# A hybrid decoder block: small matmuls of even and odd heads issued in alternation, each half in its own PSUM bank

## The chip, the cores and the metric

The kernel runs on one core of one Trainium2 chip. The metric is the device time of one execution in microseconds (us). Times of single instructions and stages come from one profiled execution of that core. TensorE is called PE, its weight loads PEld, VectorE DVE, ScalarE ACT, GpSimd POOL and SyncE SP.

## What is computed

One decoder block over 512 tokens and 16 learned meta tokens, width 1024, all in float32. A mixer runs two kinds of heads side by side, stick-breaking attention (8 heads of 64) and gated linear attention (GLA, 4 heads with keys of 64 and values of 128), and one output projection joins them. Behind it a PEER layer looks up 16 of 16384 one-neuron experts for each of 8 heads and token.

```python
# stick-breaking attention, per head
z = einsum('qd,kd->qk', q, k) * 64 ** -0.5
log_1m = where(mask, log_sigmoid(-z), 0)
between = cumsum(log_1m, reverse=True) - log_1m
a = where(mask, exp(log_sigmoid(z) + between), 0);  o = a @ v
# gated linear attention, per head and chunk
o = (q * exp(bcum)) @ state + (q k^T with decay exp(bcum_t - bcum_s), causal) @ v
state = exp(b_last) * state + (k * exp(b_last - bcum))^T @ v
# PEER
s1, s2 = q1 @ sub_keys1^T, q2 @ sub_keys2^T     # per head, 64 features, 128 keys each
top 16 of each, top 16 of the sums, softmax -> gates
y = sum_k gate_k * gelu(x . U[e_k]) * V[e_k]
```

## The kernel before

The 512 tokens are four blocks of 128 in two groups: blocks 0 to 2 (group 0) and block 3 (group 1). `front(g)` is the mixer of a group and `mid(g)` its output projection, second norm and PEER queries. `topk(blk)` scores the keys of a block and picks 16 experts a head. `spread` turns the choice of blocks 0 to 2 into dense weights (its products are line 865, between DVE's one-hots B, L859, and POOL's products Am, L861). In the last and longest part, the 128 x 128 experts run densely for blocks 0 to 2 (products of U into `pj` banks and of V into six `acc` banks, by the helper `mm3`, L187 to L189, three products of operands split in a high and a low part), while block 3 gathers its rows. Group 0 projects by `mm3` as well, group 1 by plain float32 products (L209).

Heads of 64 features lie two on 128 partitions: even heads (s = 0) on partitions 0 to 63, odd heads (s = 1) on 64 to 127. Five places multiply per half:

- `level(l)` in `gla_scores`: scores of GLA, eight levels a group, L373, 64 rows a half, into a `pz` bank per half and chunk. DVE takes each bank into `att` under a mask (L376).
- `gla_out`: per block, products of the state with the decayed queries (L430, 64 rows) and of the scores with the values (L432, 128 rows), in turn for each head, into one `pz` bank per half. `state` (L402, L406) then updates S.
- `sb_attn`, scores: per key block and group of heads a tile z (L522, 64 rows), in the query group's own blocks with a mask product of bf16 behind every score (L525, 128 rows), then `softplus` on ACT (L500 to L502) and DVE (L503), products over it (L530, L534, L537) and the exponent `a` (L540).
- `sb_attn`, sums over values: L551, 64 output columns a half, into `po` (group 0) or `pk` (group 1).
- `topk`: key scores, L716, 64 rows a half, four heads to a bank.

PSUM has eight banks. Group 0 works with 2 `pj`, 3 `pz` and 3 `po`, group 1 with 2 `pj`, 2 `pk`, 2 `pz` and 2 `px`. Tiles sp, az and a have three buffers each.

What sets the order: the code is recorded in the order in which it is written (`ORDER` for the pieces of a mixer, `SCHED` for the second group between lookups and spreading), and a scheduler of the framework then writes a fixed list for each engine from its own estimates. So rows of one tile may stand among others in an engine's list, and each engine works through its list.

## Time and profile before

| | |
|---|---|
| time, median of 3 runs | 1712.57 us (1709.4 to 1714.22) |
| span of the profiled execution | 1712.3 us |
| PE busy | 1625.8 us, 95% |
| PE weight loads busy | 1448.6 us, 85% |
| DVE busy | 1230.3 us, 72% |
| ACT busy | 703.9 us, 41% |
| POOL busy | 529.2 us, 31% |
| mean granted PE clock | 0.982 |

The page gives no time of the profiled execution other than its span. A float32 matmul shows as two instructions. The end of a matmul in the trace is modelled and lies some 0.27 us behind its start even where the next one starts after a tenth of a microsecond, so what a run of matmuls costs is read from its first start to the start of the next other instruction. Group 0's mixer fills the time from about 20 to 250 us, with its attention from 82 to 155, the levels from 173 to 202 and the GLA outputs from 214 to 232 us. Group 1, the lookups and the spreading follow until about 680 us, and the dense experts from there to the end.

### The profile page before, as it was taken

Reading aid. Unit: us, or ns where it says so; the run is one execution under the profiler, and the core shown is the slowest. Engines: PE = TensorE matmul, PEld = TensorE weight load, DVE = VectorE, ACT = ScalarE, POOL = GpSimd, SP = SyncE. Lnnn points to the kernel's source line nnn. Section 1 sums busy time; section 2 is a strip of 40 time slices with the busy share of each in tenths; the row PEclk is TensorE's granted clock in tenths of the full one; section 3 lists DMA queues with packets and bytes.
Section 4 is the critical chain, followed back from the end, with each engine's and each line's share of the span. In section 5 each row is a group of like instructions: output and inputs, shape, how many; then the busy total and the mean of one; then the engine's idle time right before and its main releaser. Section 6 shows DMA issues by size and latency. Waiting matters only on the chain.

```text
span 1712.3 us, 24535 instructions
## 1 busy us (share of the span) xinstructions
PE 1625.8 (95%) x9025; PEld 1448.6 (85%) x9025; DVE 1230.3 (72%) x2484; ACT 703.9 (41%) x1104; POOL 529.2 (31%) x401
## 2 busy tenths in 40 slices
PE   6999998988888799999999999999999999999996
PEld 5967988976678788989999999999999999999885
DVE  4225737389989998988777777777777777777674
ACT  5357355324455566333333333333333333333343
POOL 0020000002455565045434344343344443434310
PEclk9989999999999899999999999999999999999998
DMA  5210215243254345689887887887888887877653
GB/s 173 82 38 28 96 63 191 82 153 111 99 195 187 136 177 214 201 271 375 322 301 280 301 320 281 315 299 277 309 304 295 303 302 293 307 278 281 213 200 134
DMA packets 145705, 376.04 MB, mean 220 GB/s; under 512 B 13712, under 2 KB 63008, under 8 KB 142512
## 3 DMA queue, kind: packets, MB, share of 16 engines
q1 hardware_dynamic: 104112, 211.92, 36.2%
q0 software_dynamic: 36864, 134.23, 21.2%
q10 hardware_dynamic: 4608, 28.31, 4.1%
q8 instruction: 71, 1.16, 0.3%
q14 instruction: 50, 0.41, 0.1%
HBM read 345.03 MB, written 29.36 MB: 219 GB/s over the span
## 4 chain that ended last, share of the span: by engine, by line
PE 77%; DVE 14%; DMA 4%; ACT 2%; issue 1%; POOL 1%; SPq 0%; DVEq 0%; ACTq 0%; POOLq 0%
PE pj L189 12%; PE pj L187 12%; PE pj L188 12%; PE acc L188 9%; PE acc L189 9%; PE acc L187 9%; PE pk L209 3%; DVE B L859 2%; PE px L865 2%; PE pz L522 1%; PE pz L373 1%; PE pz L530 1%; DVE sc L775 1%; DMA gu<-expert_u,idx 1%; DMA vf<-expert_v 1%
## 5 line engine op out<-in xcount | busy, mean ns | idle before, releaser
L189 PE MATMUL pj<-xDh,ul 128*128 128x384 f32 x1000 | 337.3, 337 | 2.5 <-DVE ul L183 2.5
L187 PE MATMUL pj<-xDh,uh 128*128 128x384 f32 x1000 | 336.6, 337 | 0.0
L188 PE MATMUL pj<-xDl,uh 128*128 128x384 f32 x1000 | 336.2, 336 | 0.0
L188 PE MATMUL acc<-vl,wh 128*128 128x512 f32 x762 | 298.8, 392 | 2.8 <-DVE vl L183 2.8
L189 PE MATMUL acc<-vh,wl 128*128 128x512 f32 x762 | 298.6, 392 | 0.0
L187 PE MATMUL acc<-vh,wh 128*128 128x512 f32 x762 | 296.2, 389 | 0.0
L807 POOL DMA_INDIRECT gu<-expert_u,idx x128 | 189.4, 1479 | 324.2 <-DVE gu L814 183.7
L807 POOL DMA_INDIRECT gu<-expert_v,idx x128 | 178.7, 1396 | 277.2 <-DVE y L825 201.5
L182 ACT ACTIVATE uh<-uf 128x1024 fp32r<-128x1024 f32 x125 | 132.5, 1060 | 304.0 <-PE pj L188 262.4
L183 DVE TENSOR_TENSOR ul<-uf,uh 128x1024 fp32r<-128x1024 f32 x125 | 157.3, 1258 | 56.1 <-ACT uh L182 56.1
L187 PEld LDWEIGHTS pj<-xDh,uh 128*128 128x128 f32 x1000 | 188.3, 188 | 4.2
L188 PEld LDWEIGHTS pj<-xDl,uh 128*128 128x128 f32 x1000 | 188.2, 188 | 4.0
L189 PEld LDWEIGHTS pj<-xDh,ul 128*128 128x128 f32 x1000 | 188.2, 188 | 3.9 <-DVE ul L183 3.5
L188 PEld LDWEIGHTS acc<-vl,wh 128*128 128x128 f32 x762 | 143.0, 188 | 32.2 <-DVE vl L183 4.3
L189 PEld LDWEIGHTS acc<-vh,wl 128*128 128x128 f32 x762 | 143.0, 188 | 29.8
L187 PEld LDWEIGHTS acc<-vh,wh 128*128 128x128 f32 x762 | 143.1, 188 | 27.8 <-ACT vh L182 0.4
L825 DVE SCALAR_TENSOR_TENSOR y<-gu,act,y 128x1024 f32<-128x1024 f32 x128 | 163.9, 1280 | 0.5
L183 DVE TENSOR_TENSOR vl<-vf,vh 128x1024 fp32r<-128x1024 f32 x127 | 155.1, 1221 | 10.2 <-ACT vh L182 10.2
L861 POOL TENSOR_TENSOR Am<-ohu,ohl 128x512 f32<-128x512 f32 x96 | 132.6, 1399 | 95.3 <-PE px L865 57.8
L814 DVE SCALAR_TENSOR_TENSOR gu<-gu,xn 128x1024 f32<-128x1024 f32 x128 | 154.7, 1219 | 8.1 <-DMA gu<-expert_u,idx 8.1
L182 ACT ACTIVATE vh<-vf 128x1024 fp32r<-128x1024 f32 x127 | 133.0, 1047 | 16.7 <-DMA vf<-expert_v 14.4
L865 PE MATMUL px<-Am,B 128*128 128x128 f32 x768 | 105.5, 289 | 24.8 <-DVE B L859 13.2
(365 smaller groups left out, 2507.9 us busy)
## 6 DMA issues: line engine op xcount, KB each, us to landing
vf<-expert_v SPq DMA_DIRECT2D x128, 512.0 KB, 3.7
uf<-expert_ut SPq DMA_DIRECT2D x125, 512.0 KB, 5.0
wf<-w_in SPq DMA_DIRECT2D x48, 512.0 KB, 3.7
Gd<-st ACTq DMA_DIRECT2D x24, 1024.0 KB, 4.0
gt<-Gd SPq DMA_DIRECT2D x16, 1536.0 KB, 12.4
wf<-w_out SPq DMA_DIRECT2D x16, 512.0 KB, 3.7
wf<-w_pq SPq DMA_DIRECT2D x16, 512.0 KB, 3.7
h<-x SPq DMA_DIRECT2D x4, 512.0 KB, 6.5
```

What stands on the lines that cost most here:

```text
L182: A.activation(hi, src, AF.Copy)
L183: V.tensor_tensor(lo, src, hi.bitcast(F32), op=OP.subtract)
L187: T.matmul(outp, lh, rh, start=first, stop=False, skip_group_check=True)
L188: T.matmul(outp, lh, rl, start=False, stop=False, skip_group_check=True)
L189: T.matmul(outp, ll, rh, start=False, stop=last, skip_group_check=True)
L209: T.matmul(o, l, r, start=st, stop=sp, skip_group_check=True)
L807: P.indirect_dma_start(out=u, out_offset=None, in_=d[table], in_offset=bass.IndirectOffsetOnAxis(ap=col, axis=0))
L814: V.scalar_tensor_tensor(u, u, 1.0, xns[blk], op0=OP.mult, op1=OP.mult, accum_out=acts[blk][:, k:k + 1]))
L825: V.scalar_tensor_tensor(y, u, acts[blk][:, k:k + 1], y, op0=OP.mult, op1=OP.add))
L859: V.tensor_tensor(B, io4, iT[:, 1, c_].unsqueeze(2).to_broadcast(sh), op=OP.is_equal)
L861: P.tensor_tensor(Am.rearrange("p t (u l) -> p t u l", l=8), ohu[:, l_].unsqueeze(3).to_broadcast([128, 4, 16, 8]), ohl[:, l_].unsqueeze(2 ...
L865: T.matmul(p[:, j * 128:(j + 1) * 128], B[:, j], Am[:, j], start=True, stop=True)
```

## The change

The loops over heads and halves change places, so that the two halves are issued in turn, each into a bank of its own, and what reads the banks follows after both halves. In `gla_out` all state products of a block come first, then the products over the values. In `sb_attn` the masks follow the scores of both halves, and the sums over values follow the exponents of both. Nothing is computed differently. Lines move: L430 and L432 become L429 and L437, L522 and L525 become L525 and L530, L530 becomes L539, L534 and L537 become L543 and L546, L551 becomes L562, L716 becomes L727.

```diff
@@ -366,13 +366,15 @@
                     V.tensor_mul(v4(qk)[:, :, :, H:], v4(dd)[:, :, :, H:], v4(gq)[:, :, :, H:])
                     lq = rq = qk
                 for i0 in range(0, 2 * nb, ch):
-                    for s in range(2):
-                        p = pz()
-                        for j in range(ch):
-                            pr, b = items[i0 + j]
-                            T.matmul(p[:, j * 128:(j + 1) * 128],
+                    pp_ = [pz(), pz()]
+                    for j in range(ch):
+                        pr, b = items[i0 + j]
+                        for s in range(2):
+                            T.matmul(pp_[s][:, j * 128:(j + 1) * 128],
                                      lq[s * 64:(s + 1) * 64, pr, b * 128:(b + 1) * 128],
                                      rq[s * 64:(s + 1) * 64, pr, b * 128:(b + 1) * 128], start=True, stop=True)
+                    for s in range(2):
+                        p = pp_[s]
                         V.copy_predicated(att[s][:, i0 * 128:(i0 + ch) * 128].rearrange("p (i t) -> p i t", t=128),
                                           lvm[:, l:l + 1, :].to_broadcast([128, ch, 128]),
                                           p[:, :ch * 128].rearrange("p (i t) -> p i t", t=128))
@@ -421,16 +423,19 @@
             A.activation(qd, rbc, AF.Exp, scale=1.0 / 16.0)
             V.tensor_mul(qd, qd, gq)
             for b, blk in enumerate(blks):
+                pp_ = [pz(), pz()]
+                for pr in range(2):
+                    for s in range(2):
+                        T.matmul(pp_[s][:, pr * 128:(pr + 1) * 128], S[s * 64:(s + 1) * 64, pr, :],
+                                 qd[s * 64:(s + 1) * 64, pr, b * 128:(b + 1) * 128],
+                                 start=pr == 0, stop=False, skip_group_check=True)
                 for s in range(2):
-                    p = pz()
+                    p = pp_[s]
                     for pr in range(2):
                         hh = 2 * pr + s
                         i = items.index((pr, b))
-                        o = p[:, pr * 128:(pr + 1) * 128]
-                        T.matmul(o, S[s * 64:(s + 1) * 64, pr, :], qd[s * 64:(s + 1) * 64, pr, b * 128:(b + 1) * 128],
-                                 start=True, stop=False)
-                        T.matmul(o, gv[:, b, hh * 128:(hh + 1) * 128], att[s][:, i * 128:(i + 1) * 128],
-                                 start=False, stop=True)
+                        T.matmul(p[:, pr * 128:(pr + 1) * 128], gv[:, b, hh * 128:(hh + 1) * 128],
+                                 att[s][:, i * 128:(i + 1) * 128], start=False, stop=True, skip_group_check=True)
                     A.activation(go[s][:, :, b, :], p[:, :256].rearrange("p (a t) -> p a t", a=2), AF.Copy)
                 if blk < 3:
                     state(NM + b * 128, 128, gv[:, b], False)
@@ -513,17 +518,21 @@
                 nq = W - q0
                 nh = 4 if nq == 128 else 512 // nq
                 for pr0 in range(0, 4, nh):
+                    zs = [pz()[:, :nh * nq] for _ in range(2)]
+                    for i in range(nh):
+                        for s in range(2):
+                            ss_ = slice(s * 64, (s + 1) * 64)
+                            T.matmul(zs[s][:, i * nq:(i + 1) * nq], kTs[kg][ss_, pr0 + i, kb * 128:(kb + 1) * 128],
+                                     sbq[ss_, pr0 + i, q0:], start=i == 0, stop=False, skip_group_check=True)
+                    if own:
+                        for s in range(2):
+                            for i in range(nh):
+                                T.matmul(zs[s][:, i * nq:i * nq + 128], identb, maskb, start=False, stop=False,
+                                         skip_group_check=True)
+                    as_ = []
                     for s in range(2):
-                        ss_ = slice(s * 64, (s + 1) * 64)
-                        z = pz()[:, :nh * nq]
+                        z = zs[s]
                         rs = RS[:, s, pr0:pr0 + nh, q0:]
-                        for i in range(nh):
-                            zc = z[:, i * nq:(i + 1) * nq]
-                            T.matmul(zc, kTs[kg][ss_, pr0 + i, kb * 128:(kb + 1) * 128], sbq[ss_, pr0 + i, q0:],
-                                     start=i == 0, stop=False, skip_group_check=True)
-                            if own:
-                                T.matmul(zc[:, :128], identb, maskb, start=False, stop=False,
-                                         skip_group_check=True)
                         sp = spool.tile([128, 512], F32, name="sp", bufs=3)[:, :nh * nq]
                         softplus(z, nh * nq, sp)
                         old = 128 if own else 0
@@ -538,18 +547,20 @@
                                              skip_group_check=True)
                         a = spool.tile([128, 512], F32, name="a", bufs=3)[:, :nh * nq]
                         A.activation(a, z, AF.Exp)
+                        as_.append(a)
                         sp3 = sp.rearrange("p (a q) -> p a q", a=nh)
                         if own:
                             P.tensor_copy(rs[:, :, :128], sp3[:, :, :128])
                         if old < nq:
                             P.tensor_add(rs[:, :, old:], rs[:, :, old:], sp3[:, :, old:])
-                        for i in range(nh):
-                            pr = pr0 + i
-                            hh = 2 * pr + s
-                            for b in range(q0 // 128, nb):
-                                cb_ = i * nq + b * 128 - q0
-                                T.matmul(pO[b][ss_, pr * 128:(pr + 1) * 128],
-                                         vts[kg][:, kb, hh * 64:(hh + 1) * 64], a[:, cb_:cb_ + 128],
+                    for i in range(nh):
+                        pr = pr0 + i
+                        for b in range(q0 // 128, nb):
+                            cb_ = i * nq + b * 128 - q0
+                            for s in range(2):
+                                hh = 2 * pr + s
+                                T.matmul(pO[b][s * 64:(s + 1) * 64, pr * 128:(pr + 1) * 128],
+                                         vts[kg][:, kb, hh * 64:(hh + 1) * 64], as_[s][:, cb_:cb_ + 128],
                                          start=(own and b == kb and pr == 0), stop=False, skip_group_check=True)
             z = pz()[:, :W]
             for pr in range(4):
@@ -709,12 +720,14 @@
         gates[blk], sels[blk] = gate, se
         sc = mp.tile([128, 2, NH, NK], F32, name="sc")
         for hg in range(2):
+            pp_ = [bank(SCT[blk]), bank(SCT[blk])]
+            for i in range(4):
+                hh = 4 * hg + i
+                for s in range(2):
+                    T.matmul(pp_[s][:, i * 128:(i + 1) * 128], qp[s * 64:(s + 1) * 64, hh, b * 128:(b + 1) * 128],
+                             keysT[s * 64:(s + 1) * 64, hh, :], start=True, stop=True)
             for s in range(2):
-                p = bank(SCT[blk])
-                for i in range(4):
-                    hh = 4 * hg + i
-                    T.matmul(p[:, i * 128:(i + 1) * 128], qp[s * 64:(s + 1) * 64, hh, b * 128:(b + 1) * 128],
-                             keysT[s * 64:(s + 1) * 64, hh, :], start=True, stop=True)
+                p = pp_[s]
                 A.activation(sc[:, s, 4 * hg:4 * hg + 4, :].rearrange("p a b -> p (a b)"), p, AF.Copy)
         yield
         vv = mp.tile([128, 2, NH, TK], F32, name="vv")
```

The lists of PE, as the scheduler wrote them, at three places. First the first score tiles of group 0's attention. A row is line, operation, out<-operands with their numbers, and shape; `pz` with a number is a tile in a bank, `sbq` the queries, `kT0` the keys, `cb` the mask's operands. Before:

```order
L522 MATMUL pz_813<-sbq_99,kT0_100 128x128
L525 LDWEIGHTS cb_76
L525 MATMUL pz_813<-cb_76 128x128
L522 MATMUL pz_836<-sbq_99,kT0_100 128x128
L525 LDWEIGHTS cb_76
L525 MATMUL pz_836<-cb_76 128x128
```

Changed:

```order
L525 MATMUL pz_813<-sbq_99,kT0_100 128x128
L525 MATMUL pz_814<-sbq_99,kT0_100 128x128
L525 MATMUL pz_813<-sbq_99,kT0_100 128x128
L525 MATMUL pz_814<-sbq_99,kT0_100 128x128
L530 LDWEIGHTS cb_76
L530 MATMUL pz_813<-cb_76 128x128
```

Eight scores alternate between the tiles of the two halves, and the eight masks follow in a row.

Second, the later tiles of the same attention, of 384 columns (`sp` is the softplus, `a` the exponent, `RS` a running sum, `v0` the values, `hnh`, `wh` and `wl` operands of a projection). Before:

```order
L530 MATMUL pz_983<-sp_986,cf_75 128x384
L537 MATMUL pz_983<-RS_809,cf_75 128x256
L551 MATMUL po_810<-a_976,v0_101 64x128
L551 MATMUL po_811<-a_976,v0_101 64x128
L551 MATMUL po_812<-a_976,v0_101 64x128
L522 MATMUL pz_1019<-sbq_99,kT0_100 128x384
L551 MATMUL po_810<-a_994,v0_101 64x128
L551 MATMUL po_811<-a_994,v0_101 64x128
L551 MATMUL po_812<-a_994,v0_101 64x128
```

Changed:

```order
L562 MATMUL po_810<-a_961,v0_101 64x128
L562 MATMUL po_811<-a_961,v0_101 64x128
L539 MATMUL pz_948<-sp_965,cf_75 128x384
L546 MATMUL pz_948<-RS_809,cf_75 128x256
L562 MATMUL po_812<-a_961,v0_101 64x128
L525 MATMUL pz_984<-sbq_99,kT0_100 128x384
L562 MATMUL po_810<-a_973,v0_101 64x128
L562 MATMUL po_811<-a_973,v0_101 64x128
L562 MATMUL po_812<-a_973,v0_101 64x128
```

The sums of one half (a_961) stand in two pieces before those of the other (a_973), and a score of one half stands alone (pz_984): nothing alternates here.

Third, the outputs of a GLA block (`qd` decayed queries, `S` the state, `att` the scores, `gv` the values). Before, in its first block:

```order
L430 MATMUL pz_1824<-qd_1821,S_89 128x128
L432 MATMUL pz_1824<-att0_114,gv_117 128x128
L430 MATMUL pz_1824<-qd_1821,S_89 128x128
L432 MATMUL pz_1824<-att0_114,gv_117 128x128
L430 MATMUL pz_1830<-qd_1821,S_89 128x128
L432 MATMUL pz_1830<-att1_115,gv_117 128x128
```

Changed, in its last block of the group:

```order
L429 MATMUL pz_1884<-qd_1821,S_89 128x128
L429 MATMUL pz_1885<-qd_1821,S_89 128x128
L429 MATMUL pz_1884<-qd_1821,S_89 128x128
L429 MATMUL pz_1885<-qd_1821,S_89 128x128
L437 MATMUL pz_1884<-att0_114,gv_117 128x128 x2
L437 MATMUL pz_1885<-att1_115,gv_117 128x128 x2
```

State products alternate between the halves, and the products over the values stand in one row behind them.

In the levels of group 0, one chunk of six products alternates, and the other chunk's halves stand three by three with projections between them. In group 1's levels the halves alternate. Its scores alternate in the tile of its own block, and stand mostly in threes in the other tiles. Of the key scores, one bank pair of block 2 is scattered among other work, and the others alternate wholly or for the most part.

## Rows read from the trace of the kernel before

**Rows 1.** The page: span; busy time, share of the span and instructions of each engine.

```profile
span 1712.3 us, 24535 instructions
PE 1625.8 (95%) x9025; PEld 1448.6 (85%) x9025; DVE 1230.3 (72%) x2484; ACT 703.9 (41%) x1104; POOL 529.2 (31%) x401
```

**Rows 2.** Windows: length, busy PE, PEld, DVE, ACT, POOL (instructions), PEclk, DMA share, GB/s.

```profile
225.00:250.00 25.00, 24.82 (x152) 21.88 (x153) 8.69 (x13) 13.98 (x27) 0.31 (x1) 1.00 0.19 67
290.00:365.00 75.00, 72.28 (x452) 65.75 (x453) 41.97 (x163) 26.22 (x61) 0.00 (x0) 0.96 0.30 106
365.00:480.00 115.00, 99.52 (x617) 78.73 (x616) 106.30 (x466) 49.86 (x96) 31.76 (x25) 0.96 0.34 120
480.00:680.00 200.00, 172.26 (x1169) 161.69 (x1167) 181.23 (x436) 111.81 (x132) 110.94 (x79) 0.95 0.49 182
775.00:800.00 25.00, 25.00 (x128) 22.77 (x127) 22.20 (x34) 8.75 (x12) 13.63 (x9) 1.00 1.05 389
```

**Rows 3.** Timeline of PE: start, us, engine, line, operation, out<-in, shapes, count.

```profile
179.87 1.57 PE L373 MATMUL pz<-qk 64*128 64x128 f32 x18
...
221.19 0.66 PE L406 MATMUL pz<-gv,kt__1842 128*64 128x128 f32 x8
221.78 0.44 PE L187 MATMUL pj<-hnh,wh 128*128 128x384 f32 x1
...
429.02 1.16 PE L522 MATMUL pz<-sbq,kT 64*128 64x128 f32 x8
430.10 1.09 PE L551 MATMUL pk<-a,v 128*64 128x128 f32 x8
431.12 1.16 PE L522 MATMUL pz<-sbq,kT 64*128 64x128 f32 x8
...
673.46 2.06 PE L716 MATMUL px<-keysT,qp 64*128 64x128 f32 x16 [0.23 <-ACT st L866]
675.45 0.45 PE L189 MATMUL pj<-xDh,ul 128*128 128x384 f32 x1
```

**Rows 4.** Timeline of PE at the first score tiles of group 0.

```profile
81.99 0.48 PE L522 MATMUL pz<-sbq,kT 64*128 64x128 f32 x2
82.41 0.23 PE L525 MATMUL pz<-cb 128*128 128x128 bf16 x1
82.57 0.49 PE L522 MATMUL pz<-sbq,kT 64*128 64x128 f32 x2
...
87.60 1.22 PE L522 MATMUL pz<-sbq,kT 64*128 64x256 f32 x2
...
94.92 1.19 PE L530 MATMUL pz<-sp,cf 128*128 128x512 f32 x2
```

**Rows 5.** Windows of the same stretch, columns as in rows 2.

```profile
85.00:87.50 2.50, 2.50 (x9) 1.59 (x9) 0.00 (x0) 0.63 (x2) 0.00 (x0) 0.50 0.34 107
...
92.50:95.00 2.50, 2.50 (x6) 1.17 (x6) 0.00 (x0) 0.84 (x2) 0.46 (x1) 0.50 0.00 0
```

**Rows 6.** Timeline of PE between two masks of a 256-column tile.

```profile
101.75 0.23 PE L525 MATMUL pz<-cb 128*128 128x128 bf16 x1
...
102.53 0.23 PE L525 MATMUL pz<-cb 128*128 128x128 bf16 x1
```

**Rows 7.** Timeline of PE at the outputs of one GLA block.

```profile
222.84 0.48 PE L430 MATMUL pz<-qd,S 64*128 64x128 f32 x2
223.25 0.49 PE L432 MATMUL pz<-att,gv 128*128 128x128 f32 x2
...
226.08 0.61 PE L402 MATMUL pz<-cf,kd 128*128 128x128 f32 x4
```

**Rows 8.** Windows of line 373 alone: length, busy PE, PEld, PEclk, DMA share, GB/s.

```profile
155.00:290.00 135.00, 19.34 (x192) 17.26 (x192) 1.00 0.31 108
```

**Rows 9.** Groups of 400 to 470 us: line, engine, operation, tiles, shapes, count, busy, mean ns, idle before.

```profile
L503 DVE SCALAR_TENSOR_TENSOR sp<-pz,az 128x512 f32<-128x512 f32 x8 | 5.4, 681 | 0.1
L502 ACT ACTIVATE az<-az 128x512 f32<-128x512 f32 x8 | 5.0, 628 | 0.0
```

## The prediction

> **What bounds the kernel now.** I read the page first, then windows of busy time, then the timeline of TensorE (PE), one place after another. The page gives a span of 1712.3 us with PE busy for 95% of it and VectorE (DVE) for 72% [rows 1]. The reader should not stop at that average, because three stages have different limits [rows 2]. From about 25 to 290 us, the mixer of the first token group, PE is busy nearly without a gap (24.8 of 25 us in the window shown) while DVE has time to spare (8.7). From 290 to 365 us the second group starts: PE 72.3 of 75, DVE 42.0. From 365 to 680 us DVE is the fuller one: 106.3 of 115 and 181.2 of 200 us, with PE at 99.5 and 172.3. From about 775 us the dense experts keep PE at 25.0 of 25 until near the end, with the same instructions in both kernels. So a microsecond of PE that is saved before 365 us moves everything behind it, and one saved between 365 and 680 us is mostly hidden behind DVE.
>
> Next, what the small matmuls cost. A float32 matmul is two instructions in the trace. Eight instructions of one 64-row half in a row take 1.08 us from the first start to the next other start, and eight of the sums over values 1.02 us [rows 3]. Two halves in one queue can run together: eight instructions of the state update that alternate between the two column halves take 0.59 us instead of 1.02, about 55 ns a step [rows 3]. For row halves there is the level: 18 instructions in 1.57 us, about 76 ns a step, although they stand six by six in the queue, while the key scores, eight by eight, take 1.99 us for 16 [rows 3]. So TensorE already overlaps short runs of the two halves, and the long runs are where strict alternation has most to give. I price an alternating run at what one of its halves costs alone.
>
> **The change, part by part.** (a) First score tile of the first group. Before, each score is followed by a mask product, 0.58 us for the two, and the sixteen score instructions with their eight masks take from 81.99 to 87.60, 5.6 us [rows 4]. At the full clock they would be 8 x 0.58 = 4.6. Changed, the scores alternate between two banks and the masks follow in one run: 1.08 us, and for the eight masks between 0.4 (eight times some 50 ns, an estimate from the 55 ns step) and 1.3 (eight times the 0.16 us from a mask to the next score). I take 0.75, nearer to a run that doesn't change shape. That is 1.8 us, 2.8 less. There is a second part. In this alternation of 64-row scores with masks the granted clock falls to half (0.50, that is 1.2 GHz) from 85 until just past 95 us [rows 5], so about 10 us of work took twice as long as it needs, at most 5 us too much; the second product over the softplus starts only at 94.92 [rows 4]. Changed, the short run is followed by two larger scores and twelve projection products in a row, the kind of work that runs at clock 1.00 elsewhere [rows 2]. I take 3.5 of the 5; the ends are 0 and 5. Together 6.3 us (2.4 to 8).
>
> (b) The other tiles of that attention. Here the order shows that the scores do not alternate: the scheduler puts other work between the two halves, since three banks don't hold two pairs. What stays for the four 256-column tiles is that masks come in twos: score and mask take 0.78 us from mask to mask [rows 6], so 1.56 a tile, and two scores and two masks some 1.26; 1.2 us in all. The eight 384-column tiles gain nothing. The sums over values of the first pair lose about 0.65 of 2.04 us (the first two instructions run alone, the rest alternate), the two pairs of 256 columns 0.3 each, and the four pairs of 384 columns get one more change of shape each, +0.15. In all 1.8 us saved (0.5 to 3).
>
> (c) State products. Before, 64-row and 128-row products alternate: 16 instructions from 222.84 to 226.08, 3.24 us, with 0.41 us for every two [rows 7]. Changed, four pairs of state products (0.41 + 2 x 0.11 = 0.64) and then eight products over values in a row (as eight in a row above, 1.08): 1.7 us, 1.5 less. Three blocks of the first group: 4.6 us (3.2 to 4.8). PE is full there [rows 2].
>
> (d) Levels of the first group: 192 instructions, 19.34 us busy, 0.10 us each [rows 8], so 2.4 us for the 24 of a level. Changed, half of a level alternates (12 instructions, 0.86), the other half stands six by six with projections between, 0.67 to 0.86 each: 2.2 to 2.6. I take nothing (2 saved to 1.5 lost): the overlap was there already.
>
> (e) Second group until 365 us. Eight levels of eight instructions, 0.8 us each, alternate fully: 0.64, saving 1.3. Key scores of the first block: 16 instructions from 1.99 to 1.08, twice, 1.8 with one run broken in two, so 1.6. The state products of the last block 1.5, but DVE waits for the key scores rather than for these. I count 3 of 4.4 (2 to 4.4).
>
> (f) Behind 365 us. Own-block scores 2.8, other scores 1, sums 2, key scores of three blocks 3.7 (one of their runs is scattered and gains nothing): 9.5 us of PE time. DVE is busy for 92% of 115 us and 91% of 200 there [rows 2], so its work hides them; if that cover were gone they would all count. I take 1 (0 to 4).
>
> Sum: (a) to (e) 6.3 + 1.8 + 4.6 + 0 + 3 = 15.7. Some of that meets waits for weights and for DVE on the way; PE's own share of the window from 365 to 480 us, 99.5 of 115 [rows 2], is 0.865, and I let that much through: 13.6. With (f) 14.6, so 1712.3 - 14.6 = 1697.7. The profiled span and the median of the runs shown, 1712.57, agree within 0.3 us, so the forecast is 1698 us. If everything lands at its high end (8 + 3 + 4.8 + 2 + 4.4 + 4 = 26) it is 1686.
>
> **The rivals.** First, the row halves do not run together when they strictly alternate, and only the regrouping helps: (a) 5.6 becomes 16 instructions in 1.99 and masks in 0.75, 1.9 saved at full clock and 1.5 of clock, (b) 1.2, (c) 16 instructions in twice 1.08, 1.1 three times, and nothing in (e): 7.9 x 0.865 = 6.8, 1705.5 us. The level's 76 ns speaks against it; that no row shows 64-row halves in strict alternation speaks for it.
>
> Second, the front's gain doesn't reach the end, because DVE sets the second group's pace even before 365 us: a quarter of 14.6 gets through, 1709 us. For it, DVE is 91 to 92% full for 315 us [rows 2]; against it, DVE stands idle for 33 of 75 us just before, waiting.
>
> Third, slower: a pair claims both banks at once and frees them late. The first group has three banks for seven pairs, the second two for four. The second half's softplus queues behind the first on ScalarE and DVE; with three steps of 0.6 us and one of 0.68 [rows 9] that is 2.5 us during which the next pair has no bank. If PE had nothing to fill it with, 11 pairs cost 27.5 us, and 27.5 - 14.6 = 12.9 makes 1725 us. It decides from 14.6 / 11 = 1.3 us of idle PE per pair. Against it: between a score and its softplus product the new order puts the sums and products of the other half, some 3.4 us of PE work in a 384-column pair (an estimate: two scores of 1.5 times the 0.62 us that a 256-column score takes of its 0.78 [rows 6], and for each half six instructions of sums, three quarters of 1.02).
>
> Fourth, the clock. The rows show it at half just when PE worked through small pieces [rows 5]; packed pairs finish sooner and leave PE less busy, so it may fall at other places, and (a) may keep its slow stretch: 0 for the clock in (a) and about 3 us lost elsewhere, 14.6 - 3 - 3 = 8.6, 1704 us. The Trainium skill, page "TensorE: Matmul & The Clock Gate", Part 1 (The HAM clock gate), says that the throttled state is the default and that activity releases it, which would speak for this rival; the trace agrees as far as the fall at 85 us goes, and no run here shows what packed halves do to it.
>
> **How the numbers follow.** Forecast case 0.62; first rival 0.07; second 0.14; third 0.12; fourth 0.05. A difference under 0.3%, about 5 us, can't be told from none here; the bound on the faster side is 1707.4 us. Faster: 0.62 + 0.07 + 0.05 and a little of the second rival, 0.75. Within: 0.13. Slower: 0.12. The range 1687 to 1710 us holds the forecast case but for its tails, and the first, second and fourth rivals: a little over 8 in 10.
>
> **What would show it right or wrong.** Right: the first score tile of the first group takes under 2.5 us instead of 5.6 and the clock stays at 1.00 from 82 to 97 us; a block's state products take 1.7 instead of 3.2 us; 16 key score instructions take about 1.1 instead of 2.0; the first product of the second group's projections starts 10 to 14 us earlier, and so does the stage with the dense experts. Wrong: alternating instructions 112 ns apart instead of in pairs (first rival); the second group starts earlier but the dense stage does not (second); idle PE before the scores of a pair, waiting for ScalarE's exponent (third); new stretches at clock 0.50 (fourth). The forecast fails as a whole if the schedule of the second group, which is another list of instructions, costs DVE more than the front gives.

## The result: 0.5% slower

| | median of the runs | ratio to before (95% interval) | profiled span |
|---|---|---|---|
| before | 1712.57 us (5 runs) | | 1712.3 us |
| changed | 1720.0 us (5 runs) | 1.0051 (1.0037 to 1.0065) | 1720.6 us |

The forecast was 1698 us with a range of 1687 to 1710. The change is slower by about 8 us, outside the range and on the other side. One of the six runs of e17 below took 5530.9 us and is left out of its median and ratio. The page after, answering [rows 1]:

```profile
span 1720.6 us, 24532 instructions
...
PE 1608.3 (93%) x9025; PEld 1432.2 (83%) x9025; DVE 1233.7 (72%) x2484; ACT 704.0 (41%) x1104; POOL 518.2 (30%) x401
```

PE is busy for 17.5 us less than in [rows 1], and the span is 8.3 us longer. So the small matmuls did get cheaper, and PE waits more. Where it waits is in the windows of the changed kernel, columns and stretches as in [rows 2]:

```profile
225.00:250.00 25.00, 24.82 (x167) 22.75 (x164) 10.71 (x17) 16.33 (x31) 0.31 (x1) 1.00 0.25 85
290.00:365.00 75.00, 68.78 (x477) 62.75 (x476) 38.24 (x149) 24.28 (x56) 0.00 (x0) 1.00 0.33 109
365.00:480.00 115.00, 87.77 (x564) 67.40 (x563) 111.85 (x472) 47.22 (x91) 32.41 (x25) 0.94 0.32 110
480.00:680.00 200.00, 166.96 (x1145) 155.98 (x1144) 178.99 (x429) 108.28 (x129) 107.55 (x79) 0.96 0.48 175
```

From 365 to 480 us PE was busy for 99.5 us and is now for 87.8, while DVE went from 106.3 to 111.9.

**The packing itself.** The timeline of PE in the changed kernel, at the places of [rows 3, 4, 7]: first score tile with its masks, state products and products over values of one block, key scores of the first block.

```profile
82.15 1.16 PE L525 MATMUL pz<-sbq,kT 64*128 64x128 f32 x16
83.24 0.62 PE L530 MATMUL pz<-cb 128*128 128x128 bf16 x8
...
221.76 0.71 PE L429 MATMUL pz<-qd,S 64*128 64x128 f32 x8
222.41 1.16 PE L437 MATMUL pz<-att,gv 128*128 128x128 f32 x8
...
329.99 1.16 PE L727 MATMUL px<-keysT,qp 64*128 64x128 f32 x16
```

Sixteen scores take 1.1 us and the eight masks some 0.6, where [rows 4] had 5.6 for both, in part at half clock. The state products of a block take 0.65 and those over the values some 1.1, against 3.24 in [rows 7]. Sixteen key scores take about 1.1 us. The 1.99 us of [rows 3] is a run of block 3, eight by eight; at this place, the first block, the list of before already mixes the halves, and the gain is smaller:

```profile
336.20 1.71 PE L716 MATMUL px<-keysT,qp 64*128 64x128 f32 x16
```

Single starts in the trace stand 6 or 7 ns apart within a pair of halves and 105 between most pairs.

**The front.** The attention's last products over the exponent tile `a` start at 138.08 instead of 151.42 us, but the first level starts at 172.73 instead of 173.22. First the two rows of before, then those of the changed kernel:

```profile
151.42 2.94 PE L569 MATMUL po<-a,vbd 128*128 128x128 f32 x24
...
173.22 1.60 PE L373 MATMUL pz<-qk 64*128 64x128 f32 x18
```

```profile
138.08 2.94 PE L580 MATMUL po<-a,vbd 128*128 128x128 f32 x24 [0.40 <-ACT a L577]
...
172.73 1.60 PE L373 MATMUL pz<-qk 64*128 64x128 f32 x18
```

The lead of 13 us is gone in 35 us. Part of it was never there: the attention ends with 408 projection products done instead of 432, and 24 products of about 0.18 us (4.3 us) now follow behind it. Most of the rest is lost in one gap of PE:

```profile
154.45 0.34 PE L188 MATMUL pj<-hnl,wh 128*128 128x400 f32 x1
155.78 0.45 PE L187 MATMUL pj<-hnh,wh 128*128 128x400 f32 x1 [0.99 <-ACT gq L341]
156.06 0.35 PE L188 MATMUL pj<-hnl,wh 128*128 128x400 f32 x1
159.19 0.70 PE L189 MATMUL pj<-hnh,wl 128*128 128x400 f32 x1 [2.78 <-DVE wl L183]
```

The product at 159.19 needs the low part `wl` of the key projection's weights, which DVE splits off. DVE's timeline of the changed kernel shows what stands ahead of that in its list: the norm of the attention's output (L594, L183 into oT0l) and the decays (L334, L337).

```profile
153.63 0.86 DVE L594 SCALAR_TENSOR_TENSOR a<-po,gsb,a 128x128 f32<-128x128 f32 x3
154.40 1.13 DVE L337 TENSOR_TENSOR_SCAN bc<-dd 128x16 f32<-128x16 f32 x4
155.45 0.55 DVE L334 SCALAR_TENSOR_TENSOR dd<-dd,qk 128x400 f32<-128x400 f32 x1
156.28 0.69 DVE L183 TENSOR_TENSOR oT0l<-a,oT0h 128x512 fp32r<-128x512 f32 x1 [0.28 <-ACT oT0h L182]
156.89 1.13 DVE L337 TENSOR_TENSOR_SCAN bc<-dd 128x16 f32<-128x16 f32 x4
157.94 2.33 DVE L183 TENSOR_TENSOR wl<-wf,wh 128x1024 fp32r<-128x1024 f32 x2
```

And behind the gap PE's granted clock is at half (windows of the changed kernel, columns as above):

```profile
155.00:160.00 5.00, 1.44 (x4) 1.10 (x5) 4.72 (x10) 2.29 (x5) 0.00 (x0) 0.80 0.32 116
160.00:165.00 5.00, 5.00 (x17) 5.00 (x17) 3.49 (x6) 3.35 (x5) 0.00 (x0) 0.51 0.98 370
165.00:170.00 5.00, 5.00 (x30) 5.00 (x28) 1.40 (x2) 1.87 (x4) 0.00 (x0) 1.00 0.30 101
```

Idle time of 3.6 us in the first window and half speed in the second come to some 6 us, with the moved products 10 of the 13. The transposes behind the output projection (L672, now L683) start at 283.74 instead of 288.25, 4.5 us earlier: 0.5 were left at the levels, and the rest comes with the state products. In the expectations below this mark is called the first output projection product.

**The second group.** It starts 4.5 us earlier and ends later: the first product into the `acc` banks comes at 736.7 instead of 732.1 us. From there to the end it takes 983.9 instead of 980.2 us, and the new list has 24 more products of U, the size of one U phase, behind that mark; e2 below, with the same list, needs 980.4 us for this part, so they need not cost. In waits of PE from 365 to 480 us (us in total, times, longest), the line of the softplus product stands out, after and before:

```profile
PE pz L539 <- DVE sp L508: 12.4, 4, 4.5
```

```profile
PE pz L530 <- DVE sp L503: 1.7, 3, 0.8
```

One of the four, on PE and on DVE of the changed kernel:

```profile
433.25 1.28 PE L878 MATMUL px<-Am,B 128*128 128x128 f32 x10
439.08 1.22 PE L539 MATMUL pz<-sp,cf 128*128 128x512 f32 x1 [4.55 <-DVE sp L508]
```

```profile
434.21 2.37 DVE L755 TENSOR_TENSOR cand<-vv 128x128 f32<-128x128 f32 x7
436.50 0.28 DVE L773 CAST fi<-iu 128x256 f32<-128x256 uint32 x1
436.70 0.68 DVE L872 TENSOR_TENSOR B<-io,iT 128x512 f32<-128x512 f32 x1
437.30 0.31 DVE L762 MAX8 tv<-cand 128x8 f32<-128x50 f32 x2
...
438.36 1.26 DVE L508 SCALAR_TENSOR_TENSOR sp<-pz,az 128x512 f32<-128x512 f32 x2
```

```profile
434.62 1.15 ACT L507 ACTIVATE az<-az 128x512 f32<-128x512 f32 x2
```

PE has nothing else ahead of that product in its list, and on DVE the softplus of block 3 stands behind pieces of the lookup (L755, L762) and of the spreading (L872). ScalarE is done with `az` of both halves at 435.8 us, so 2.6 of the 4.55 us are DVE's order. DVE works through another list. In this window it also takes longer for two of its forms: `sc<-fp,df` 372 instead of 286 ns (32 times) and B 876 instead of 768 ns (17 times), together 4.6 of the 5.5 us that it is busier. That isn't what the slower kernels share: in e7 and e10 below, with losses of the same order, DVE is busy in this window for as long as its instructions would be at the mean that each form has before, within 0.5 us.

### The profile page after: what moved, and what is told of

Read it like the earlier page. It is cut to its first block, busy times and chain, and to the rows that moved or that the text cites. A ratio compares the mean times of both kernels' runs of the same rounds, so it can differ in the third digit from the quotient of the medians.

```text
span 1720.6 us, 24532 instructions
## 1 busy us (share of the span) xinstructions
PE 1608.3 (93%) x9025; PEld 1432.2 (83%) x9025; DVE 1233.7 (72%) x2484; ACT 704.0 (41%) x1104; POOL 518.2 (30%) x401
## 4 chain that ended last, share of the span: by engine, by line
PE 79%; DVE 13%; DMA 5%; ACT 2%; issue 1%; POOL 0%; SPq 0%; DVEq 0%; ACTq 0%; POOLq 0%
PE pj L187 12%; PE pj L189 12%; PE pj L188 12%; PE acc L188 9%; PE acc L189 9%; PE acc L187 9%; PE px L878 3%; DVE B L872 2%; PE pk L209 2%; PE pz L373 1%; PE pz L539 1%; DMA vf<-expert_v 1%; PE pz L525 1%; DVE sc L788 1%; DMA wf<-w_out 1%
## 5 line engine op out<-in xcount | busy, mean ns | idle before, releaser
L820 POOL DMA_INDIRECT gu<-expert_u,idx x128 | 183.2, 1431 | 334.4 <-DVE gu L827 193.0
L183 DVE TENSOR_TENSOR ul<-uf,uh 128x1024 fp32r<-128x1024 f32 x125 | 157.9, 1263 | 56.2 <-ACT uh L182 56.2
L183 DVE TENSOR_TENSOR vl<-vf,vh 128x1024 fp32r<-128x1024 f32 x127 | 154.9, 1220 | 11.2 <-ACT vh L182 11.2
L182 ACT ACTIVATE vh<-vf 128x1024 fp32r<-128x1024 f32 x127 | 133.1, 1048 | 21.1 <-DMA vf<-expert_v 19.8
```

The lines of the kernel that those rows point to most:

```text
L182: A.activation(hi, src, AF.Copy)
L183: V.tensor_tensor(lo, src, hi.bitcast(F32), op=OP.subtract)
L820: P.indirect_dma_start(out=u, out_offset=None, in_=d[table], in_offset=bass.IndirectOffsetOnAxis(ap=col, axis=0))
```

## The experiments

All are compared with the kernel before on the same chip; groups of runs were on different chips, so between them the ratio tells more than the median. PE idle is 510 us less PE's busy time in the window from 290 to 800 us, of the one profiled execution.

| kernel | median, us | ratio (95% interval) | PE idle, us |
|---|---|---|---|
| before | 1712.6 to 1714.2 | | 50.1 |
| whole change | 1720.0 | 1.0051 (1.0037 to 1.0065) | 72.1 |
| e1 first group | 1708.05 | 0.9975 (0.9960 to 0.9991) | 51.2 |
| e2 second group and keys | 1722.0 | 1.0065 (1.0043 to 1.0086) | 65.5 |
| e3 change, h loads off SP | 1719.53 | 1.0039 (1.0020 to 1.0058) | 67.9 |
| e4 before, h loads off SP | 1713.2 | 1.0005 (0.9989 to 1.0021) | 51.1 |
| e5 state products of group 0 alone | 1706.22 | 0.9960 (0.9941 to 0.9979) | 48.6 |
| e6 e1, decays ahead of attention | 1714.67 | 1.0004 (0.9989 to 1.0020) | 50.5 |
| e7 e1 and all key scores | 1725.53 | 1.0063 (1.0045 to 1.0081) | 66.8 |
| e8 e1 and block 3's attention | 1710.93 | 0.9986 (0.9971 to 1.0000) | 63.3 |
| e9 e1, keys hold two banks, not alternating | 1708.24 | 0.9967 (0.9952 to 0.9982) | 52.0 |
| e10 e1 and keys of blocks 0, 3 | 1721.56 | 1.0042 (1.0024 to 1.0059) | 62.0 |
| e11 e1 and keys of blocks 1, 2 | 1712.75 | 0.9986 (0.9971 to 1.0002) | 56.1 |
| e12 e1, norm behind levels | 1702.6 | 0.9928 (0.9915 to 0.9942) | 53.2 |
| e13 e5, norm behind levels | 1709.36 | 0.9970 (0.9958 to 0.9983) | 50.3 |
| e14 whole change, norm behind levels | 1712.91 | 1.0000 (0.9987 to 1.0013) | 68.7 |
| e15 e12, level and states of block 3 | 1701.47 | 0.9934 (0.9915 to 0.9953) | 51.6 |
| e16 e14 and one more U phase | 1719.91 | 1.0036 (1.0020 to 1.0052) | 73.7 |
| e17 e15, keys partly overlapped | 1699.35 | 0.9925 (0.9895 to 0.9954) | 49.4 |
| e18 e15, keys alternating | 1714.79 | 1.0010 (0.9993 to 1.0027) | 63.1 |

### Which half costs: e1 and e2

The written loops of before and after both stand in the kernel, chosen by the group (`g == 0` in e1; `g == 1` in e2, with the key scores as in the change). The lists of the two runs are those of before and after, joined at about 290 us.

```diff
+                    if g == 0:
+                        pp_ = [pz(), pz()]
...
+                    else:
                         for s in range(2):
                             p = pz()
```

> The change in the first group alone: level, attention and state products of blocks 0 to 2 alternate as in the changed kernel; the second group and the key scores are written as before. The lists of all engines then read as after up to about 290 us and as before behind that. Theory A (the front gains some 4.5 us at 290 us and the second group's new list is what costs time): the first output projection product comes at 283 to 285 us instead of 288.2, the second group keeps its list, and the end lies 3 to 6 us before that of the kernel before, 1706.5 to 1709.5. Rival B (the second group's pace doesn't depend on when it starts, DVE sets it): 1711 to 1714. Rival C (an earlier start collides with something, whatever the list of the second group): slower than before, 1715 to 1720.

> The other half alone: level, attention and state products of block 3 and the key scores of all blocks alternate, the first group is written as before. The lists read as before up to about 290 us and as after behind that. Theory A (the second group's new list is what costs): first output projection product at 288 us as before, the early U products and the first dense experts late, and an end 8 to 13 us behind the kernel before, 1720 to 1726. Rival B or C (the list itself costs nothing): the packed key scores and states save what they save on PE, 1709 to 1713.

The windows from 290 to 800 us, first e1, then e2:

```profile
290.00:800.00 510.00, 458.82 (x2852) 412.88 (x2851) 443.41 (x1394) 232.23 (x344) 183.00 (x125) 0.97 0.50 180
```

```profile
290.00:800.00 510.00, 444.50 (x2798) 399.65 (x2799) 434.39 (x1391) 228.82 (x347) 164.56 (x120) 0.95 0.49 173
```

Theory A holds: the first group gains 0.25%, the second costs 0.65%, and the two together (0.4%) agree with the whole within the intervals. The gain of the front does reach the end, in the second group's old list. In the new one PE is idle for 14 us more.

### What eats the attention's lead: e3, e4, e5, e6

On SP, the loads of h stand ahead of weight loads in the changed kernel and wait 18 us for a buffer. My first suspect was this queue.

```diff
-            nc.sync.dma_start(h[:, b], d["x"][blk * 128:(blk + 1) * 128, :])
+            (nc.gpsimd if g == 0 else nc.sync).dma_start(h[:, b], d["x"][blk * 128:(blk + 1) * 128, :])
```

> The changed kernel with one edit: the loads of the residual input h of the first group are issued from GpSimd instead of SP. The lists of PE and DVE are the same. Theory A (weights for the gate and value projections wait on SP behind an h load, which waits until 157 us for a buffer): the next weight loads are issued from about 140 us, the first level product comes at 160 to 169 us instead of 172.7, the first output projection product at 276 to 281 instead of 283.7, and 2 to 7 us of it reach the end: 1713 to 1718. Rival (the chain of the decays through ScalarE and DVE sets the levels anyway): first level product within 1 us of 172.7 and an end within 1.5 us of the changed kernel's 1720.0.

> The kernel before with the same edit alone: h loads of the first group issued from GpSimd. There the four weight loads stand ahead of the h loads on SP, so by theory A little is to be had: first level product within 1 us of 173.2, end 1710 to 1713.5. Rival (the h loads hold up SP in any order): levels 3 us earlier or more, end 1706 to 1710.

The suspicion fell. In e3 the first level starts at 173.51 us, the same wait for `wl` of 2.8 us is in the trace, and the time is that of the changed kernel within its interval. In e4 the time is that of before; its levels start 2.8 us earlier, but its attention already ended that much earlier.

> Only the state products and the products over values of the first group are regrouped; everything else is written as before, and of all lists only 24 products on PE stand in another place. Theory A (the attention's lead of 13 us is lost again before the levels, so what reached the second group in the run with the whole first group is the regrouped products alone): the first output projection product comes 4 to 5 us earlier than in the kernel before, the levels start as before, and the end is that of the whole first group, 1707 to 1710. Rival (attention's part does reach the end, about half of the 5.7 us): 1710 to 1712.

The state products alone give 0.4%, no less than the whole first group in e1 (0.25%, overlapping intervals). So no worth of the attention's packing shows there, and the front's gain in e1 can be term (c) alone. The median of 1706.2 lies just below the range of theory A.

The profile of e5 shows one thing more. Up to the state products it has the instructions of before, yet from its first score to its last products over `a` the attention takes 66.5 us (81.07 to 147.58) instead of 69.4 (81.99 to 151.42), with the clock at half for a shorter time than in [rows 5]. Windows of e5, columns as above:

```profile
85.00:87.50 2.50, 2.50 (x13) 1.41 (x13) 0.56 (x1) 1.71 (x4) 0.00 (x0) 0.94 0.59 203
87.50:90.00 2.50, 2.50 (x8) 1.56 (x7) 0.82 (x2) 1.50 (x3) 1.22 (x2) 0.50 0.02 7
90.00:92.50 2.50, 2.50 (x10) 1.13 (x9) 0.42 (x1) 1.28 (x3) 0.00 (x0) 0.87 0.00 0
```

In e4 and e13, with the same attention, it takes 67.8 us. So how long this stretch lasts differs between executions, and the 55.9 us of the changed kernel (82.15 to 138.08) are a gain of 10.6 us on e5 instead of 13.5 on before.

For e6 the gate projection and the decays were written as a piece of their own (d), ahead of the attention (a):

```diff
-ORDER = ("nqaylvorx", "nlvorxqay")
+ORDER = ("nqdaylvorx", "nlvorxqay")
```

> The first group packed as a whole, and the gate projection with the chain of decays (two products, three ScalarE steps, scans on DVE) written ahead of the attention instead of behind it; the second group is written as before and its lists are the same. Theory A (the levels wait for this chain, which starts only behind the attention): first level product at 160 to 167 us instead of 172.5, first output projection product 6 to 11 us earlier than the 283.9 of the run with the first group alone, end 1698 to 1704. Rival (the levels wait for PE itself, for the projections that feed them, and for the last weights): first level product at 170 us or later and an end of 1706 to 1710.

The levels start at 165.07, as theory A asked, but the time is that of before, above the range of either theory. PE now waits among the levels for DVE's qk (4.6 us), and its clock falls there. Windows of e6, columns as above:

```profile
170.00:175.00 5.00, 2.84 (x32) 2.49 (x33) 4.92 (x10) 3.94 (x5) 0.00 (x0) 1.00 0.66 252
175.00:180.00 5.00, 4.95 (x37) 4.65 (x35) 4.19 (x9) 1.69 (x2) 0.00 (x0) 0.53 0.00 0
...
190.00:195.00 5.00, 5.00 (x31) 4.55 (x29) 2.60 (x6) 0.00 (x0) 0.00 (x0) 0.50 0.31 105
195.00:200.00 5.00, 5.00 (x30) 4.55 (x30) 3.07 (x6) 0.00 (x0) 0.00 (x0) 0.50 0.30 107
200.00:205.00 5.00, 5.00 (x27) 4.78 (x27) 2.23 (x5) 0.00 (x0) 0.00 (x0) 0.50 0.00 0
```

The clock is at half until about 206 us. From 175 to 290 us its mean is 0.87, which is 15 us of full speed missing, and the transposes start at 289.89. So the chain of decays was not the reason, or not by itself.

### The gap closed: e12, e13, e14

What is left is DVE's order, with the norm ahead of the split of the weights. Written behind the levels (y behind l), the norm moves 20 instructions on PE and some 60 on DVE, and nothing in the second group.

```diff
-ORDER = ("nqaylvorx", "nlvorxqay")
+ORDER = ("nqalyvorx", "nlvorxqay")
```

> The first group packed; the norm of the attention's output is written behind the levels instead of ahead of them, so that on DVE the split of the key projection's weights and the decays stand ahead of it. PE's list is the same but for 20 instructions, the second group's lists are the same. Theory N (PE waits 3.8 us at 155 to 159 us because the split of the weights stands behind the norm on DVE, and its clock falls for the 5 us after): no such wait, first level product at 163 to 168 us instead of 172.5, first output projection product at 275 to 280 instead of 283.9, end 1699 to 1705. Rival (the levels are held up on DVE later, as in the run with the decays ahead of the attention): levels begin earlier but the output projection does not, 1706 to 1714.

The gap is gone and the clock stays, with the first level 10 us earlier (windows and timeline of e12):

```profile
155.00:160.00 5.00, 5.00 (x30) 5.00 (x29) 1.23 (x1) 1.89 (x3) 0.00 (x0) 1.00 0.52 186
160.00:165.00 5.00, 4.73 (x43) 4.23 (x42) 4.23 (x7) 1.83 (x3) 0.00 (x0) 1.00 0.37 129
```

```profile
162.52 1.60 PE L374 MATMUL pz<-qk 64*128 64x128 f32 x18
```

The transposes start at 278.46, 5 us before those of e1, and the median is 5.5 us less (0.47% by the ratios). Theory N holds. About half of the 10 us is lost again behind the levels: from 175 to 290 us PE is idle for 7.6 us instead of 4.2 and the mean clock is 0.96.

> State products of the first group regrouped and the norm written behind the levels, attention and levels as before. Theory (the attention's packing is worth some 6 us of its own once the levels don't wait): the move alone gains little, since in the kernel without packed attention PE has no gap at 155 us; first level product at 169 to 174 us, end 1704 to 1708. Rival (the moved norm gains by itself, the attention's packing is still worth nothing): first level product at 160 to 166 us, end 1700 to 1704.

> The whole change, with the norm written behind the levels; nothing else differs from the changed kernel, and its second group's lists are the same. Theory (front and second group are separate): the front's repair passes on, 5 to 7 us less than the changed kernel, 1713 to 1716, PE idle from 290 to 800 us still about 70 us. Rival (the loss of the second group depends on when it starts): within 2 us of 1720, or below 1709.

Moving the norm without packing the attention gains nothing (1709.36 against 1706.22 in e5, intervals overlap; the end and the first level, at 167.62, lie 1.4 us outside the theory's ranges). With it, the packed attention is worth 0.42% (e12 against e13), about 7 us, and 8.1 x 0.865 = 7.0 is what the forecast had for (a) and (b). And the whole change with the norm moved is 7 us faster than without, while its second group keeps its loss: front and second group are separate.

### What in the second group costs: e7 to e11

> The first group packed, and the key scores of all four blocks in pairs; level, attention and states of block 3 as before. Theory A1 (a pair of key scores claims both banks that block 3's attention also uses, and the list places them late or scattered): most of the 11 us that the second group's part costs show here, 1714 to 1720. Theory A2 (the attention pairs of block 3 cost it): 1705 to 1710, since the key scores save up to 3.7 us of PE.

> The first group packed, and the attention of block 3 in pairs; its level and states and all key scores as before. Theory A1 (the key scores cost): 1705 to 1710. Theory A2 (the attention pairs of block 3 cost, since a pair waits until both of two banks are free): 1714 to 1720. Should the two only cost together, both runs stay below 1711.

> The first group packed, and the key scores claim both banks at once as in the change, but the sixteen products run half by half as before (eight of one half, then eight of the other). The lists of DVE, ScalarE and SP are the same as in the run with the first group alone, and on PE only the key scores themselves stand elsewhere. Theory L (the cost of the packed key scores lies in the other list of the second group that comes with them): 1706 to 1710, as the first group alone. Rival H (a pair that holds both banks costs by itself): 1713 to 1720.

In e9 both banks are claimed first, and the halves run one after the other:

```diff
+            pp_ = [bank(SCT[blk]), bank(SCT[blk])]
             for s in range(2):
-                p = bank(SCT[blk])
                 for i in range(4):
                     hh = 4 * hg + i
-                    T.matmul(p[:, i * 128:(i + 1) * 128], ...
+                    T.matmul(pp_[s][:, i * 128:(i + 1) * 128], ...
...
```

> The first group packed, and key scores alternating in blocks 0 and 3 alone, whose banks nothing of block 3's attention uses. Theory L (each variant has its own list, and its cost doesn't follow from what is packed): another list than either neighbour, anywhere from 1705 to 1726. Theory A1 (the cost comes from the banks shared with block 3's attention): 1704 to 1709, with the saving of these two blocks.

> The other half: key scores alternating in blocks 1 and 2 alone, whose banks block 3's attention uses too. Theory A1 (shared banks): most of the cost of all key scores, 1718 to 1726. Theory L (the list): anywhere from 1705 to 1726, and the two half runs don't add up to the whole.

Windows from 290 to 800 us of e9 and of e10:

```profile
290.00:800.00 510.00, 457.97 (x2828) 412.19 (x2826) 439.17 (x1390) 230.00 (x340) 177.62 (x123) 0.96 0.50 176
```

```profile
290.00:800.00 510.00, 448.00 (x2788) 402.25 (x2788) 431.02 (x1378) 226.91 (x337) 161.86 (x120) 0.97 0.48 171
```

Key scores in pairs cost 0.9% on top of e1 (e7), more than theory A1 asked for. That is not because a pair holds two banks: e9 holds them in the same way, with the lists of e1 on all engines but for the key scores' own places, and has e1's time. Nor is it the banks that blocks 1 and 2 share with block 3's attention: theory A1 asked for most of the loss in e11, and it came in e10, whose key scores share nothing with the attention. The attention pairs of block 3 alone (e8) make PE wait 9.4 us for their softplus between 365 and 480 us, and PE is idle for 63 us in an execution of 1721.1 us that was the longest of its runs; the median lies only 2.9 us over e1, with overlapping intervals. Theory L let e10 and e11 come out anyhow, and said that they wouldn't add up; in fact they add up, 0.8% over e1 against 0.9% in e7, and nearly all of it is blocks 0 and 3. What e10, e7 and the whole change have in common is another list of the second group and 11 to 21 us more of idle PE than e1. Another list alone need not cost: by the order of starts in the traces, key scores left aside, e9 has PE's and DVE's order of e1 exactly, e10 moves some 360 matmuls on PE and 610 instructions on DVE, but e8 moves 390 and 400 and e11 360 and 180, and these two cost 0.1%, within the intervals. It depends on which list comes out.

### A better kernel, and a last test: e15 to e18

> The first group packed with the norm behind the levels, and level and state products of block 3 packed as well; its attention and the key scores as before. Some 70 instructions of PE and 30 of DVE stand elsewhere than in the best kernel so far (1702.6). Theory (these stand before 365 us and leave the later lists alone): key scores of the second block 1 to 2.5 us earlier than there, end 1700 to 1703. Rival (any packing in the second group costs): 1706 or more.

Level and state products of block 3, which stand before 365 us and move some 100 instructions, cost nothing; the saving is within the intervals.

> As e14, and one more U phase of the dense experts is placed into the second group's work (4.2 us of PE). Theory (PE idles there for want of work that is ready): the phase fills idle time and the end comes 2 to 4 us earlier than in e14. Rival (DVE sets the pace there, and the phase's split of weights takes its time from the lookups): within 1.5 us of e14, or later.

One more U phase among the spreading makes it 7 us worse, against the theory: PE is idle for 74 us. The list around it changed again, so the run doesn't tell whether PE idles for want of ready work; it shows that a piece more of it doesn't fill the gaps.

> The kernel of 1701.5 us (norm behind the levels; first group, level and states of block 3 packed), with the key scores of a pair in the sequence of halves 0 0 0 1 0 1 1 1, so that they overlap in the middle. Apart from the key scores themselves some 30 instructions of PE and 30 of DVE stand elsewhere. Theory L (only the list costs): sixteen products in 1.3 to 1.6 us instead of 2.0, PE idle from 290 to 800 us about 52 us, end 1699 to 1703. Rival (overlapping key scores cost by themselves): 1707 or more.

> The same kernel with key scores in strict alternation 0 1 0 1, where the second group's lists come out otherwise (some 700 instructions on PE). Theory L: sixteen products in 1.2 us, PE idle from 290 to 800 us 60 us or more, and 8 to 16 us more than 1701.5, 1709 to 1717. Rival (the loss seen before belonged to the unrepaired front): 1699 to 1704.

The sequence of halves and heads in e18 (removed lines, halves in turn) and in e17:

```diff
-            for i in range(4):
...
-                for s in range(2):
+            for s, i in ((0, 0), (0, 1), (0, 2), (1, 0), (0, 3), (1, 1), (1, 2), (1, 3)):
```

Key scores of the first block and the window from 290 to 800 us, first of e17, then of e18:

```profile
327.24 1.49 PE L767 MATMUL px<-keysT,qp 64*128 64x128 f32 x16
```

```profile
290.00:800.00 510.00, 460.60 (x2875) 414.26 (x2875) 440.30 (x1397) 232.88 (x344) 183.39 (x127) 0.98 0.53 183
```

```profile
326.19 1.16 PE L767 MATMUL px<-keysT,qp 64*128 64x128 f32 x16
```

```profile
290.00:800.00 510.00, 446.89 (x2795) 401.68 (x2795) 428.29 (x1383) 226.66 (x335) 180.96 (x123) 0.97 0.51 177
```

With the old list the kernel stays at 1699 us (1701.5 in e15, intervals overlap); with the new one PE is idle for 13.7 us more (63.1 against 49.4), and the median is 15.4 us more. In PE's waits from 290 to 800 us, some 14 us more in e18, only 4 are ahead of the key scores themselves (4.7 against 0.9, for ScalarE and DVE); the others are ahead of products that the edit doesn't touch. The saving at stake is small: all key scores together are busy for 14.8 us in e15, 14.1 in e17 and 12.9 in e18. Since e17 overlaps only in part (one run of sixteen in block 3 still takes 2.06 us), full alternation with the old list has not been run.

## Why the forecast was wrong, step by step

**(a), (b): near in size, in part by luck, and wrong in reach.** The first tile takes 1.1 + 0.6 us (1.8 forecast) and the clock stays at 1.00 from 75 to 100 us in e1, against the stretch at half in [rows 5]. The attention ends 13.3 us earlier, of which 4.3 are projection products moved behind it: 9.0, where 8.1 were priced. The clock's 3.5 us were read from one execution with a long stretch at half: on e5 the gain is 10.6, less the moved products 6.3. Of the lead, 0.5 us reached the levels and next to none the second group, since DVE's list then made PE wait for `wl`. The step that failed is the pass-through: I took it from PE's share of a later window (0.865), and didn't ask what the products behind the attention wait for once they come earlier. e12 and e13 show that it is worth 7 us with the norm out of the way.

**(c): right.** 1.7 us a block as forecast, and in e5 alone 0.4% (0.2 to 0.6), where 4.6 x 0.865 = 4 us is 0.23%.

**(d): right.** Levels of the first group are busy for 20.1 us after, 19.34 in [rows 8], within the range given; the clock is 1.00 from 173 to 202 us in the changed kernel and in [rows 8].

**(e), (f): the prices on PE were near in sum, the cover was not.** Key scores were priced at 1.6 + 3.7 = 5.3 us, from block 3's run of 1.99, and save 3.2 (busy for 15.6 us before, 12.4 after; 1.9 from e15 to e18), since the old list mixes the halves at other places. Scores, masks and sums of block 3's attention save 7.1 (21.1 to 13.9), where 5.8 were priced. But the term (f), "1 (0 to 4)" saved, was in truth a loss of some 12 us (whole change against e1; e2 against before: 8 to 11). I let DVE's work hide the saving, as if the rest stayed in its order. It didn't: the fixed lists of the second group were written anew, and PE waits more in them. My text named this in its last sentence as what would make the forecast fail, and gave it no chance and no price of its own; the 0.12 for a slower result belonged to the third rival. That omission is what left the true time outside the range.

**The rivals.** The first fell with the 6 ns between the halves. The second holds in part: the second group starts earlier and the dense stage does not, but e1 shows that an earlier start does pass through the old list. The third had the sign and a wait of the kind, PE idle in block 3's attention; its reason, that a pair holds both banks, fell with e9 for the key scores, and e8 shows that the wait alone costs little. The fourth was right about one new stretch at half clock (160 to 165 us), some 2.5 us, and the old one at 85 us went.

**What stays open.** Which property of the new list costs the 12 us isn't settled. e9, e17 and e18 show that it comes with the list and not with the banks; e8 against e10 shows that it is no single wait, since the waits sit elsewhere in each list. Added up from 290 to 800 us, three waits of PE are longer in each of the changed kernel, e7, e10 and e18 than in e1: for DVE's one-hots B 15.9 to 18.5 us instead of 10.3, for the weights of the input projection 7.4 to 13.5 instead of 4.9, and for `ul`, which DVE splits off, 4.6 to 5.9 instead of 2.5. In e17, with the old list, they are 13.8, 7.6 and 2.7, so the weights don't tell the lists apart; whether B or `ul` sets the time isn't shown. That the loss would vanish with full alternation in the old list is argued, not shown.

## What to carry to other kernels

When an edit goes through a scheduler that writes the whole order, price two things apart: what the edited instructions cost, which rows read at the same place give well, and what the rest of the order becomes, which no row of before gives; the second needs a chance of its own, on the slow side as well. Try such an edit place by place and keep those that leave the later lists alone: here state products, attention and levels, 0.7% faster, while the key scores cost more than the whole saves. And before counting on a lead, find the next instruction that the earlier work will wait for: here it stood on another engine behind a norm that nothing needed yet.

## What the runs showed of the hardware

Two 64-row halves of a float32 matmul in strict alternation start 6 to 7 ns apart, so sixteen instructions take 1.1 us where eight by eight took 1.99 (block 3 before, 673.46 us); the sequence 0 0 0 1 0 1 1 1 overlaps in part (1.49 us as the timeline groups it). Eight bf16 masks in a run start every 55 ns.

The granted clock fell to half (1.2 GHz) behind 3.6 us of idle PE and came back after some 6 us of large projection products (the changed kernel at 155 to 165 us). In e6 it fell at about 175 us, behind 2.2 us of idle PE, and stayed at half for some 30 us of level products, although PE shows as busy throughout the last 16 of these. The same level products run at full clock when no such gap comes just before them (173 to 202 us in the changed kernel). In the attention of before the clock is at half for 10 us from 85 us on while PE shows as busy; in e5, with the same instructions, for about 3.5 us.
